# Gate on the accumulators between the third and the fourth step of a Strassen-type second projection, and the residual added in the fourth

## The chip, the core and the metric

The kernel runs on one core of one Trainium2 chip. The time is the device time of one execution in microseconds (us). The kernel before takes 2689.62 us, the median of three runs (2686.9 to 2690.53). TensorE multiplies matrices and writes to PSUM, VectorE, ScalarE and GpSimd (POOL in the rows) do the element-wise work, and all loads and stores are issued by SyncE's queue (SP).

## The reference

One decoder layer on 2048 rows of 1024 columns. The change touches the MLP behind the mixer; `x` is the normed row entering it, `gt2`, `sh2`, `sc2` come from the conditioning vector.

```python
x = layer_norm(ALPHA * x + gt1 * y, ln1_g, ln1_b)
h = x * (1.0 + sc2) + sh2
f = jnp.square(jax.nn.relu(h @ w_ff1)) @ w_ff2        # 1024 -> 4096 -> 1024
x = layer_norm(ALPHA * x + gt2 * f, ln2_g, ln2_b)
```

All of it is float32. The kernel reaches that accuracy with three matmuls for one: each operand is split into a rounded high part and the rest (`split`: ScalarE writes the high part, VectorE or GpSimd subtracts), and `mm3` multiplies high x high, low x high and high x low.

## The kernel before

The work on the MLP is cut into two halves of 1024 rows (`for half`). Each half goes through the first projection; after both, each goes through the second.

Both projections are multiplied as 2x2 blocks with seven products in place of eight (Strassen in Winograd's form): P1 to P7 are products of blocks or of sums and differences of blocks, and the four blocks of the result are sums of some of them. So P1 goes into block (0,0), and into others through the running sums.

**First projection** (`up`, lines 1058 to 1120). 16 blocks `c` of 256 of the 4096 columns run per half, in pairs that take turns product by product (`next(pair[y])`). A block has four PSUM banks X, Y, Z, W. In the order P1 P5 P6 P7 P3 P4 P2, X takes P1 and P2, Z takes P5 and P3, Y takes P6, W takes P7 and P4. Line 1098 copies X to `u`, line 1101 adds Y, line 1105 forms `v = u + Z` before P3 is added into Z, line 1108 adds W before P4 goes into W, and lines 1113 and 1118 form two more results. `act` applies ReLU and the square and writes to DRAM (`g_d`). The weight's four blocks are loaded raw, added or subtracted on GpSimd (line 1076; on VectorE for the first four blocks of columns) and split into `wh` and `wl`, of which the pool `w1p` holds five each. The activations' seven operands are made by `split_h`, which a loop runs through before the first block is traced; each has its own pool (`hs4`), and the string `HSO` gives the order in which the pools of this stage are opened. Pools are stacked in memory, so this order decides which tiles of the stage before (`p3`: the output projection with its layer norm, whose statistics lie in `sm3`) a pool's tiles lie over, and so what they wait for.

Beside this the second weight is prepared (`prep`, line 1124): 16 pieces of 1 MB are loaded, combined and split into the seven operands of each of four steps `s` (1024 of the 4096 rows each), and written to DRAM (`wt_d`). A list of slots spreads the pieces over the blocks.

**Second projection** (`down`, from line 1239 on). Per half, four steps `s` of seven products; a product is two half-products of 24 matmuls, and PSUM holds four row tiles of it at a time. For each half-product a weight operand is loaded (`wl`, five buffers), the activation operand is formed by a subtraction (line 1259) and split (`gp`, three buffers). Line 1297 adds each row tile of each product to an accumulator in SBUF (8 tiles of 128x1024, in 4 blocks or quarters `(i, j)` of 4 row tiles x 512 columns); line 1295 copies the first of them. In the last step the order is P1 P5 P6 P3 P2 P7 P4, else P7 stands before P2.

After the last step come, per row tile, the gate (line 1213), the residual (`residual`: a load of `z`, two operations on GpSimd, and the add of line 1214), the layer norm's statistics (line 189), and the output. In the last step of the second half four tiles are normalized on VectorE (lines 1227 and 1230), the others on ScalarE (1234) and GpSimd or VectorE (1235, 1236). For its last product P4, the gate and residual of tiles 4 to 7 are applied ahead, and the product is multiplied by the gate on its way (line 1280).

The order of each engine's instructions is chosen when the kernel is built, by a planner that goes by the order in which they are traced as priority and by its own estimate of durations. Each engine then executes its list in order. `tc.issue_after(wdma[-1])` puts a load into SP's queue behind the last weight load traced.

Of the kernel before, what the change touches and what calls it, by code (L numbers as in the profile page):

```python
# [51 lines left out]
HSO = 6, 4, "u", 5, 3, 2, "s", "o", 0, 1, "w"  # L52
# [7 lines left out]
WLS = "VV"  # L60
WOS = "wwww", "xxzz"
# [9 lines left out]
OV = 4  # L71
GB = 3
WLB = 5
PIECES = 8 * 7
OO = 2
# [42 lines left out]
def build(nc, tc, I, out, upto=9, dbg=None):  # L118
# [805 lines left out]
    p3 = ctx.enter_context(ExitStack())  # L924
    h2p = pool(p3, "h2p", 2)
# [9 lines left out]
    sm3 = pool(p3, "sm3", 4)  # L935
# [84 lines left out]
    p4 = ctx.enter_context(ExitStack())  # L1020
    psf = [pool(p4, f"psf{i}", 4, space=PSUM) for i in range(2)]


    p4a = p4.enter_context(ExitStack())
# [13 lines left out]
    def split_h(half, o):  # L1038
# [5 lines left out]
        for x, (name, src, sub) in enumerate((("P1", b11, None), ("P5", b12, (b12, b11)), ("P6", b12, (b22, b12)),  # L1044
                                              ("P7", b11, (b12, b11)), ("P3", b22, None), ("P4", b12, (b21, b12)),
                                              ("P2", b21, None))):
# [11 lines left out]
    def up(half, c, H):  # L1058
# [9 lines left out]
        for _ in range(n // 2 % 4):  # L1068
            x, z, y, w = (order.index(i) for i in "XZYW")
            order[y], order[z], order[w], order[x] = "X", "Z", "Y", "W"  # L1070
# [36 lines left out]
        prod("P3", a21, OP.subtract, "Z", False, (a12, a21))  # L1107
        V.tensor_tensor(v, v, ps["W"], op=OP.add)
        act(v, 1, 1)
        yield  # L1110
# [4 lines left out]
        yield  # L1115
        prod("P2", a12, None, "X", False)
# [3 lines left out]
        act(ps["X"], 0, 0)  # L1120
# [3 lines left out]
    def prep(u):  # L1124
        s, k = divmod(u, 4)
        b = hraw.tile([P, 2, D], F32, tag="raw", name=f"w2r{u}")
        Q.dma_start(b, I["w_ff2"][8 * s * P:(8 * s + 8) * P].rearrange("(i k p) c -> k p i c", i=2, p=P)[k])
        b11, b12, b21, b22 = (b[:, i, 512 * j:512 * j + 512] for i in range(2) for j in range(2))
# [15 lines left out]
    for _ in split_h(0, H):  # L1144
        pass
    for half in range(2):
        todo = work(range(8 * half, 8 * half + 8))
        slots = [i for i in range(7 * NCH) if half or i < 7 * NCH - 8]
        slots = slots[14:] if half else slots[12:]
        want = PIECES  # L1150
# [3 lines left out]
        for c in range(0, NCH, 2):  # L1154
            pair = [up(half, x, H) for x in (c, c + 1)]
            for x in range(7):
                for y in range(2):
# [31 lines left out]
    ztp = pool(p4b, "ztp", 2)  # L1189
    sm4 = pool(p4b, "sm4", 4)  # L1190
    NST = DFF // 1024
    acc = {}
    wdma = []
    gt2, ag1, ab1, g2, b2 = (c4.tile([P, D], F32, name=n) for n in ("gt2", "ag1", "ab1", "g2", "b2"))
    rows = (gt2, gt_d[1]), (ag1, I["ln1_g"]), (ab1, I["ln1_b"]), (g2, I["ln2_g"]), (b2, I["ln2_b"])
# [8 lines left out]
    def residual(half, t):  # L1204
        zt = ztp.tile([P, D], F32, tag="zt", name=f"zt{half}_{t}")
        with tc.issue_after(wdma[-1]):
            Q.dma_start(zt, z_d[4 * border[2 * half + t // 4] + t % 4])
# [8 lines left out]
    def finish(half, t):  # L1216
        tt = 4 * border[2 * half + t // 4] + t % 4
        f = acc[t]
        if half == 0 or t < 4:
            gate(f, residual(half, t))  # L1220
# [161 lines left out]
```

## Time and profile before

| what | us |
|---|---|
| median of three runs | 2689.62 |
| profiled execution | 2691.44 |
| its span, first to last instruction | 2689.6 |
| TensorE busy (matmul) | 2447.0 (91%) |
| VectorE busy | 1815.3 (67%) |
| ScalarE busy | 1209.6 (45%) |
| GpSimd busy | 1148.1 (43%) |
| mean granted clock of TensorE | 0.96 |
| first matmul of the first projection | 1301.6 |
| first matmul of the second projection | 1982.75 |

Busy time is the sum of the instructions' durations on an engine; it says nothing on whether the engine could have done without waiting, so the stages are read one by one in the rows below. In a row, the operation stands as `out<-in` by tile names: `u_X` is bank X of the first projection, `d_W` bank W of the second, `acc` an accumulator, `zt` the residual, `gt` the gate, `w2s` a piece of the second weight, `a` a raw activation block of the second projection.

### The profile page before, as it was taken

Reading aid. Unit: us, or ns where it says so; the run is one execution under the profiler, and the core shown is the slowest. Engines: PE = TensorE matmul, PEld = TensorE weight load, DVE = VectorE, ACT = ScalarE, POOL = GpSimd, SP = SyncE. Lnnn points to the kernel's source line nnn. Section 1 sums busy time; section 2 is a strip of 40 time slices with the busy share of each in tenths; the row PEclk is TensorE's granted clock in tenths of the full one; section 3 lists DMA queues with packets and bytes.
Section 4 is the critical chain, followed back from the end, with each engine's and each line's share of the span. In section 5 each row is a group of like instructions: output and inputs, shape, how many; then the busy total and the mean of one; then the engine's idle time right before and its main releaser. Section 6 shows DMA issues by size and latency. Waiting matters only on the chain.

```text
span 2689.6 us, 33970 instructions
## 1 busy us (share of the span) xinstructions
PE 2447.0 (91%) x11668; PEld 2028.9 (75%) x11668; DVE 1815.3 (67%) x2891; ACT 1209.6 (45%) x2349; POOL 1148.1 (43%) x1055
## 2 busy tenths in 40 slices
PE   5999999989999999799799998989989999799982
PEld 5887878877787877588587786867878887588871
DVE  8657675566767776644877649776445557965578
ACT  5653222257777777234565555655542112221110
POOL 4323546558788977333312336323300004810037
PEclk9999999989999999899899999999999999899995
DMA  9366341020202111556688626886266767476552
GB/s 325 139 218 203 106 137 37 32 80 23 64 20 60 33 49 57 168 179 227 222 300 281 225 102 206 304 277 226 102 256 247 301 252 267 179 291 261 191 188 78
DMA packets 203469, 464.71 MB, mean 173 GB/s; under 512 B 18584, under 2 KB 52760, under 8 KB 188960
## 3 DMA queue, kind: packets, MB, share of 16 engines
q1 hardware_dynamic: 203296, 462.54, 49.4%
q8 instruction: 92, 1.51, 0.2%
q14 instruction: 81, 0.66, 0.1%
HBM read 313.30 MB, written 149.17 MB: 172 GB/s over the span
## 4 chain that ended last, share of the span: by engine, by line
PE 62%; DVE 16%; DMA 10%; issue 5%; ACT 4%; POOL 2%; SPq 0%; DVEq 0%; ACTq 0%; POOLq 0%
DMA wt_d<-w2s 4%; PE d_W L132 4%; PE d_W L133 4%; PE d_W L134 4%; PE t L835 3%; DMA wad<-in_w_ada 2%; PE o L826 2%; PE o L828 2%; PE d_Z L134 2%; PE d_Z L133 2%; PE pj L134 2%; PE d_Z L132 2%; PE pj L132 2%; PE pj L133 2%; PE s L132 2%
## 5 line engine op out<-in xcount | busy, mean ns | idle before, releaser
L1076 POOL TENSOR_TENSOR w<-w,w 128x512 f32<-128x512 f32 x112 | 167.7, 1503 | 377.7 <-DVE w1l_P L129 234.2
L129 DVE TENSOR_TENSOR w1l_P<-w,w1h_P 128x512 fp32r<-128x512 f32 x224 | 194.6, 872 | 65.7 <-ACT w1h_P L126 64.4
L807 ACT ACTIVATE p<-s,nm 128x512 f32<-128x512 f32 (+3 forms) x320 | 196.6, 627 | 39.7 <-DVE nm L804 36.2
L802 DVE TENSOR_REDUCE mx<-s 128x1 f32<-128x512 f32 (+3 forms) x288 | 175.2, 620 | 54.0 <-PE s L134 51.2
L1208 POOL TENSOR_TENSOR zt<-zt,ag 128x1024 f32<-128x1024 f32 x16 | 44.1, 2762 | 355.6 <-DMA zt<-z_d 355.6
L851 POOL TENSOR_TENSOR tl<-tf,th 128x512 fp32r<-128x512 f32 x144 | 183.7, 1288 | 1.7
L126 ACT ACTIVATE w1h_P<-w 128x512 fp32r<-128x512 f32 x224 | 138.1, 622 | 97.4 <-PE u_Y L133 25.2
L835 PE MATMUL t<-ident,p 128*128 128x128 f32 x1088 | 165.0, 277 | 7.8 <-DVE tl L129 4.0
L835 PEld LDWEIGHTS t<-ident,p 128*128 128x128 f32 x1088 | 130.6, 142 | 33.0 <-ACT tf L846 6.1
L133 PE MATMUL pj<-wbl,hhb 128*128 128x512 f32 x384 | 151.3, 394 | 0.6 <-DVE wbl L129 0.6
L132 PE MATMUL pj<-wbh,hhb 128*128 128x512 f32 x384 | 150.8, 395 | 0.9 <-ACT wbh L126 0.5
L134 PE MATMUL pj<-wbh,hlb 128*128 128x512 f32 x384 | 151.4, 395 | 0.0
L132 PE MATMUL s<-kt,qt 96*128 96x512 f32 (+3 forms) x320 | 128.4, 401 | 12.4 <-ACT p L807 10.2
L129 DVE TENSOR_TENSOR w2s<-w2r,w2s 128x512 fp32r<-128x512 f32 x112 | 98.0, 876 | 57.7 <-ACT w2s L126 57.2
L132 PE MATMUL u_Z<-hh_P,w1h_P 128*128 128x512 f32 x256 | 104.9, 410 | 28.4 <-DVE v L1105 28.4
L826 PE MATMUL o<-th,v 128*128 128x512 f32 (+2 forms) x320 | 123.1, 389 | 5.0 <-DVE osum L862 4.2
L828 PE MATMUL o<-tl,v 128*128 128x512 f32 (+2 forms) x320 | 124.0, 396 | 3.2 <-DVE tl L129 1.8
L126 ACT ACTIVATE w2s<-w2r 128x512 fp32r<-128x512 f32 x112 | 70.2, 628 | 123.7 <-DMA wt_d<-w2s 103.9
L133 PE MATMUL s<-kt,qt 96*128 96x512 f32 (+3 forms) x320 | 118.8, 371 | 3.7 <-DVE kt L129 3.7
L134 PE MATMUL s<-kt,qt 96*128 96x512 f32 (+3 forms) x320 | 118.5, 371 | 0.0
L132 PE MATMUL psY<-wo_h,mh 128*128 128x512 f32 x256 | 101.1, 400 | 10.8 <-ACT wo_h L126 10.3
L129 DVE TENSOR_TENSOR tl<-t,th 128x512 fp32r<-128x512 f32 (+3 forms) x176 | 92.7, 539 | 26.9 <-ACT th L126 25.7
(377 smaller groups left out, 7750.0 us busy)
## 6 DMA issues: line engine op xcount, KB each, us to landing
wP<-wt_d SPq DMA_DIRECT2D x112, 1024.0 KB, 4.8
wt_d<-w2s SPq DMA_DIRECT2D x112, 512.0 KB, 3.9
w<-in_w_ff SPq DMA_DIRECT2D x128, 256.0 KB, 3.8
a<-g_d SPq DMA_DIRECT2D x32, 1024.0 KB, 7.2
g_d<-v SPq DMA_DIRECT2D x96, 256.0 KB, 4.5
wad<-in_w_ada SPq DMA_DIRECT2D x64, 256.0 KB, 3.0
w2r<-in_w_ff SPq DMA_DIRECT2D x16, 1024.0 KB, 7.1
x<-in_x SPq DMA_DIRECT2D x16, 512.0 KB, 7.9
```

The lines of the kernel that those rows point to most:

```text
L126: A.activation(hi, x, AF.Copy)
L129: lo_eng.tensor_tensor(lo, x, hi.bitcast(F32), op=OP.subtract)
L132: T.matmul(ps, sh, mh, start=start, stop=False, skip_group_check=more)
L133: T.matmul(ps, sh, ml, start=False, stop=False, skip_group_check=more)
L134: T.matmul(ps, sl, mh, start=False, stop=stop, skip_group_check=more)
L802: V.tensor_reduce(mx[:, j:j + 1], ps[:, :n], op=OP.max, axis=AX.X)
L807: A.activation(pt[:, :m], b[:, :m], AF.Exp, bias=nm, accum_out=rs[:, qi, j:j + 1])
L826: T.matmul(po[:, cs], w, th[:, cs], start=(done == 0), stop=False)
L828: T.matmul(po[:, cs], w, tl[:, cs], start=False, stop=(done == nk))
L835: T.transpose(tp[:, qi * P:(qi + 1) * P], pts[h, 4 * qb + qi, kb // 4][1][:, kb % 4 * P:(kb % 4 + 1) * P], ident)
L851: (V if mode == "C" else G).tensor_tensor(tl[:, cs], tf[:, cs], th[:, cs].bitcast(F32), op=OP.subtract)
L1076: (V if half == 0 and c < W1V else G).tensor_tensor(src, *sub, op=op)
```

## The change

It has five parts.

1. *Gate.* `gt2` is loaded when the MLP begins. Each quarter of the accumulators is multiplied by it once, in the step before the last, behind the product that completes the quarter there. What the last step adds must then be gated already: its weight rows (`s == NST - 1`) are multiplied by `gt2` column by column in `prep`.
2. *Residual.* In the last step, behind P1, P5, P6 and P3, the residual of one quarter each is loaded, scaled on GpSimd and added to the accumulators, in pieces of 128x512 (four buffers) in place of 128x1024 (two).
3. The special path for the last P4 loses its gate, and `finish` begins with the statistics. The order "row tile by row tile" of P4's matmuls stays.
4. *Order of the first projection.* P2 goes ahead of P3 and P4: P1 P5 P6 P7 P2 P3 P4. The banks' order for the next block, the pools' order and two buffer counts (v 4 to 3, r 2 to 1) go with it.
5. *Entry.* The seven operands of the first half are traced one by one, each ahead of the product that needs it in the first pair of blocks. `sm3` is opened as the first pool of the stage before. The last weight pieces are to be finished ten slots earlier.

```diff
-HSO = 6, 4, "u", 5, 3, 2, "s", "o", 0, 1, "w"
+HSO = 6, 5, "u", 4, 3, 2, "s", "o", 0, 1, "w"
+RES = dict(P1=(0, 1), P5=(1, 1), P6=(0, 0), P3=(1, 0))
-OV = 4
+OV = 3
-OO = 2
+OO = 1
...
     p3 = ctx.enter_context(ExitStack())
+    sm3 = pool(p3, "sm3", 4)
...
-    sm3 = pool(p3, "sm3", 4)
...
+    gt2p = pool(p4, "gt2p", side="right")
+    gt2 = gt2p.tile([P, D], F32, name="gt2")
+    rowbc(gt2, gt_d[1])
...
-            order[y], order[z], order[w], order[x] = "X", "Z", "Y", "W"
+            order[y], order[x], order[z], order[w] = "X", "Z", "Y", "W"
...
+        prod("P2", a12, None, "X", False)
         V.tensor_tensor(v, v, ps["W"], op=OP.add)
         act(v, 1, 1)
+        yield
+        prod("P3", a21, OP.subtract, "Z", False, (a12, a21))
+        act(ps["X"], 0, 0)
         yield
         prod("P4", a22, None, "W", False)
...
+        if s == NST - 1:
+            for i in range(2):
+                V.tensor_tensor(b[:, i], b[:, i], gt2, op=OP.mult)
+            yield
...
-    for _ in split_h(0, H):
-        pass
+    first = split_h(0, H)
...
-        slots = slots[14:] if half else slots[12:]
-        want = PIECES
+        slots = slots[14:-10] if half else slots[12:]
+        want = 8 * 7 + 4 * half
...
+                if half == 0 and c == 0:
+                    next(first, None)
...
+    def quarter(half, i, tp, j):
+        return acc[4 * i + tp][:, 512 * j:512 * j + 512]
+
+    def gate(half, i, j):
+        for tp in range(4):
+            c = quarter(half, i, tp, j)
+            V.tensor_tensor(c, c, gt2[:, 512 * j:512 * j + 512], op=OP.mult)
+
+    def residual(half, i, j):
+        cs = slice(512 * j, 512 * j + 512)
+        for tp in range(4):
+            zt = ztp.tile([P, 512], F32, tag="zt", name=f"zt{half}_{i}{j}{tp}")
+            with tc.issue_after(wdma[-1]):
+                Q.dma_start(zt, z_d[4 * border[2 * half + i] + tp][:, cs])
+            G.tensor_tensor(zt, zt, ag1[:, cs], op=OP.mult)
+            G.tensor_tensor(zt, zt, ab1[:, cs], op=OP.add)
+            c = quarter(half, i, tp, j)
+            V.tensor_tensor(c, c, zt, op=OP.add)
...
     def finish(half, t):
-        if half == 0 or t < 4:
-            gate(f, residual(half, t))
...
             if half == 1 and last and name == "P4":
                 ops = [parts(q) for q in range(2)]
                 for tp in range(4):
-                    gate(acc[4 + tp], residual(half, 4 + tp))
-                for tp in range(4):
                     for k in range(4):
                         mm(tp, k, *ops[k // 2])
-                    y = ztp.tile([P, D], F32, tag="zt", name=f"y{tp}")[:, 0:512]
-                    V.tensor_tensor(y, ps[ch, tp], gt2[:, 0:512], op=OP.mult)
-                    V.tensor_tensor(acc[4 + tp][:, 0:512], acc[4 + tp][:, 0:512], y, op=OP.add)
-                return
...
+                if s == NST - 2 and (name, i, j) in (("P2", 0, 0), ("P3", 0, 1), ("P7", 1, 1), ("P4", 1, 0)):
+                    gate(half, i, j)
+            if last and name in RES:
+                residual(half, *RES[name])
```

## Rows read from the trace of the kernel before

**Rows 1.** Table of stretches: length, busy us per engine (count), granted clock, DMA share, GB/s.

```profile
1700.00:1800.00 100.00, 89.11 (x380) 72.64 (x379) 76.54 (x102) 55.24 (x99) 25.03 (x16) 0.96 0.83 283
...
2250.00:2360.00 110.00, 88.32 (x347) 69.59 (x347) 101.07 (x90) 31.03 (x35) 87.18 (x41) 0.91 0.61 224
...
2474.00:2549.00 75.00, 75.00 (x333) 62.10 (x332) 42.02 (x48) 14.07 (x14) 0.00 (x0) 1.00 0.54 197
...
2549.00:2604.00 55.00, 55.00 (x244) 45.56 (x243) 38.50 (x44) 11.99 (x12) 12.87 (x7) 1.00 0.59 211
...
2604.00:2622.00 18.00, 10.84 (x48) 8.63 (x46) 18.00 (x14) 1.95 (x2) 12.46 (x5) 0.89 0.32 114
...
2622.00:2636.00 14.00, 13.63 (x48) 10.93 (x48) 14.00 (x13) 0.00 (x0) 13.92 (x8) 0.78 0.12 40
...
2636.00:2690.00 54.00, 0.26 (x2) 0.00 (x0) 45.87 (x46) 3.61 (x3) 34.52 (x22) 0.52 0.23 87
```

**Rows 2.** Timeline of TensorE, 2614 to 2623 us: start, length, instruction, [idle before].

```profile
2614.46 0.39 PE L134 MATMUL d_W<-wP,gP7l 128*128 128x512 f32 x1
...
2622.37 0.77 PE L132 MATMUL d_W<-wP,gP4h 128*128 128x512 f32 x1 [7.53 <-issue]
```

**Rows 3.** Timeline of VectorE, end of the last step.

```profile
2621.61 0.66 DVE L1297 TENSOR_TENSOR acc<-acc,d_W 128x512 f32<-128x512 f32 x1
...
2685.13 1.40 DVE L1230 SCALAR_TENSOR_TENSOR acc<-acc,rs,b 128x512 f32<-128x512 f32 x2
```

**Rows 4.** Groups by form, 2592 to 2690 us: busy us, mean ns, idle before.

```profile
L1214 DVE TENSOR_TENSOR acc<-acc,zt 128x1024 f32<-128x1024 f32 x8 | 18.2, 2276 | 4.6 <-POOL zt L1209 4.5
L1213 DVE TENSOR_TENSOR acc<-acc,gt 128x1024 f32<-128x1024 f32 x8 | 17.1, 2158 | 0.0
...
L1280 DVE TENSOR_TENSOR y<-d_W,gt 128x512 f32<-128x512 f32 x4 | 2.7, 684 | 0.1
...
L189 DVE BATCH_NORM_STATS2 st<-acc 128x6 f32<-128x512 f32 x16 | 10.1, 674 | 0.0
```

**Rows 5.** Instructions on the accumulators: ns shortest/median/longest, first and last start.

```profile
L1297 DVE TENSOR_TENSOR acc<-acc,d_W x100: 625/687/689, 2037.2 to 2623.5; 128x512 f32<-128x512 f32 x100
...
L1213 DVE TENSOR_TENSOR acc<-acc,gt x16: 1210/1933/3422, 2260.3 to 2631.7; 128x1024 f32<-128x1024 f32 x16
...
L1227 DVE SCALAR_TENSOR_TENSOR acc<-acc,mv,g x8: 737/740/2831, 2640.3 to 2684.5; 128x512 f32<-128x512 f32 x8
```

**Rows 6.** Waits of TensorE, 1280 to 1980 us: total, times, longest.

```profile
PE u_Z L132 <- DVE v L1105: 28.4, 7, 7.2
...
PE psT L965 <- ACT z L1001: 12.8, 2, 8.6
```

**Rows 7.** Timeline of VectorE and TensorE at 1798 us.

```profile
1798.05 0.68 DVE L1105 TENSOR_TENSOR v<-u,u_Z 128x512 f32<-128x512 f32 x1
...
1798.87 0.77 PE L132 MATMUL u_Z<-hh_P,w1h_P 128*128 128x512 f32 x1 [5.17 <-DVE v L1105]
```

**Rows 8.** Waits of ScalarE, 1300 to 1980 us.

```profile
ACT w2s L126 <- DMA wt_d<-w2s: 103.9, 67, 4.5
```

**Rows 9.** Instructions of line 1076 on GpSimd.

```profile
L1076 POOL TENSOR_TENSOR w<-w,w x112: 1280/1519/2381, 1375.5 to 1940.6; 128x512 f32<-128x512 f32 x112
```

**Rows 10.** Timeline of SP's queue, from 2538 us.

```profile
2538.72 38.40 SPq L1257 DMA_DIRECT2D wP<-wt_d  x8
```

**Rows 11.** Groups by form, 2236 to 2362 us, the change of half.

```profile
L1259 DVE TENSOR_TENSOR a<-a,a 128x1024 f32<-128x1024 f32 x8 | 20.7, 2605 | 0.0
...
L1213 DVE TENSOR_TENSOR acc<-acc,gt 128x1024 f32<-128x1024 f32 x8 | 15.1, 1908 | 0.0
```

**Rows 12.** Groups by form, 1980 to 2236 us.

```profile
L1259 DVE TENSOR_TENSOR a<-a,a 128x1024 f32<-128x1024 f32 x31 | 37.7, 1224 | 1.7 <-DMA a<-g_d 1.0
```

**Rows 13.** Timeline of ScalarE at the entry.

```profile
1299.55 1.24 ACT L1001 ACTIVATE z<-z,nm,rs 128x1024 f32<-128x1024 f32 x1 [4.12 <-DVE nm L200]
...
1300.70 2.17 ACT L126 ACTIVATE w1h_P<-w 128x512 fp32r<-128x512 f32 x4
```

More of the change, by code (lines that the diff above doesn't have):

```diff
@@ L70 @@
 W1B = 5
-OV = 4
+OV = 3
 GB = 3
 WLB = 5
-PIECES = 8 * 7
-OO = 2
+OO = 1
 W1U = 2
@@ L1020, in build @@
     p4 = ctx.enter_context(ExitStack())
+    NST = DFF // 1024
     psf = [pool(p4, f"psf{i}", 4, space=PSUM) for i in range(2)]
+    gt2p = pool(p4, "gt2p", side="right")
+    gt2 = gt2p.tile([P, D], F32, name="gt2")
+    rowbc(gt2, gt_d[1])
     p4a = p4.enter_context(ExitStack())
@@ L1044, in split_h @@
         for x, (name, src, sub) in enumerate((("P1", b11, None), ("P5", b12, (b12, b11)), ("P6", b12, (b22, b12)),
-                                              ("P7", b11, (b12, b11)), ("P3", b22, None), ("P4", b12, (b21, b12)),
-                                              ("P2", b21, None))):
+                                              ("P7", b11, (b12, b11)), ("P2", b21, None), ("P3", b22, None),
+                                              ("P4", b12, (b21, b12)))):
             p = hs4[x]
@@ L1106, in up @@
         yield
-        prod("P3", a21, OP.subtract, "Z", False, (a12, a21))
+        prod("P2", a12, None, "X", False)
         V.tensor_tensor(v, v, ps["W"], op=OP.add)
         act(v, 1, 1)
+        yield
+        prod("P3", a21, OP.subtract, "Z", False, (a12, a21))
+        act(ps["X"], 0, 0)
         yield
@@ L1114, in up @@
         act(v, 0, 1)
-        yield
-        prod("P2", a12, None, "X", False)
         v = o("v", "v")
@@ L1119, in up @@
         act(v, 1, 0)
-        act(ps["X"], 0, 0)
     def prep(u):
@@ L1188, in build @@
     wl = pool(p4b, "wl", WLB)
-    ztp = pool(p4b, "ztp", 2)
+    ztp = pool(p4b, "ztp", 4)
     sm4 = pool(p4b, "sm4", 4)
-    NST = DFF // 1024
     acc = {}
     wdma = []
-    gt2, ag1, ab1, g2, b2 = (c4.tile([P, D], F32, name=n) for n in ("gt2", "ag1", "ab1", "g2", "b2"))
-    rows = (gt2, gt_d[1]), (ag1, I["ln1_g"]), (ab1, I["ln1_b"]), (g2, I["ln2_g"]), (b2, I["ln2_b"])
+    ag1, ab1, g2, b2 = (c4.tile([P, D], F32, name=n) for n in ("ag1", "ab1", "g2", "b2"))
+    rows = (ag1, I["ln1_g"]), (ab1, I["ln1_b"]), (g2, I["ln2_g"]), (b2, I["ln2_b"])
     def load_rows():
@@ L1202, in load_rows @@
             G.tensor_scalar(t, t, ALPHA, 0.0, op0=OP.mult, op1=OP.add)
[L1204 to L1207, printed above, removed]
-        G.tensor_tensor(zt, zt, ag1, op=OP.mult)
-        G.tensor_tensor(zt, zt, ab1, op=OP.add)
-        return zt
-    def gate(f, zt):
-        V.tensor_tensor(f, f, gt2, op=OP.mult)
-        V.tensor_tensor(f, f, zt, op=OP.add)
+    def quarter(half, i, tp, j):
[14 more added lines that the diff above has]
+            V.tensor_tensor(c, c, zt, op=OP.add)
     def finish(half, t):
```

## The prediction

> **What bounds the kernel now.** I read the table of stretches first. From 2474 to 2604 us TensorE is busy in all of the time at granted clock 1.00, the upper of its two levels, 2.4 GHz [rows 1]; there nothing but fewer matmuls could shorten the span. 333 recorded matmuls in 75 us are 0.225 us each. The second projection loses time mostly in two places. Around the change of half (2250 to 2360) 347 matmuls, 78 us of work, take 110 us: 32 us lost, with VectorE busy in 101 and GpSimd in 87. At the end TensorE stops at 2614.7, waits 7.5 us, runs 14 us for its last 48 matmuls at mean clock 0.78, and from 2636 to the end only VectorE and GpSimd work [rows 1, 2].
>
> Next I read what VectorE does there. It adds the seventh product's first tile at 2621.6 [rows 3] although TensorE had it done at 2614.7, and the fourth product, which adds into the same bank, starts right behind, at 2622.4 [rows 2]. So VectorE's backlog is the bound from about 2605 on: 8 gate multiplies, 17.1 us, and 8 residual adds, 18.2 us, with the 8 statistics pairs and the output's multiplies behind them [rows 4]. The gate multiply takes 1.21 us at its fastest and 3.42 at its slowest; the add of a PSUM bank never takes over 0.689 [rows 5]. So an operation whose two inputs lie in SBUF is stretched when GpSimd works, and one with a PSUM input is not.
>
> For the first projection I read TensorE's waits: 28.4 us in seven waits for line 1105, the longest 7.2 us at the entry, and 12.8 us at the entry for the layer norm before it [rows 6]. At 1798 line 1105 runs in VectorE's order behind the splits of the second weight [rows 7], whose ScalarE half waits 103.9 us in all for the write of an earlier piece [rows 8].
>
> **The end of the last step.** Gate multiplies (17.1 us) and residual adds (18.2 us) leave VectorE's last 90 us, and the four multiplies with the gate of line 1280 (2.7 us) go too [rows 4]: 38 us, and the wait for GpSimd's residual operand with it. Then the backlog is gone and the fourth product follows the seventh at once: 2614.8 + 48 x 0.225 = 2625.6. What remains late is the chain per row tile: add 0.69, two statistics 2 x 0.67, aggregate 0.2: 2.2 us, and for the three tiles finished on VectorE four operations of 0.74 more [rows 4, 5]: 5.2 us. The product completes its row tiles one by one, 2.7 us apart, the first at 2617.5; VectorE needs 2.2 + 3 x 5.2 = 17.8 us and ends at 2635.3, plus 3 for the first four tiles' remains and for the multiply of the one tile on GpSimd beside them, plus 3.1 from VectorE's last operation (2686.5) to the end: 2641 to 2642 against 2689.6. Gain 48, I take 47 (bounds 35, if GpSimd stretches all twelve operations as now, and 51).
>
> **The residual in the fourth step.** It doesn't vanish: per half 16 loads of 256 KB, 32 GpSimd operations on 128x512 and 16 adds. GpSimd's nearest row is 1.28 us at its fastest, 1.52 median [rows 9]: 41 to 49 us. The weight loads run five buffers ahead in SP's queue (eight issued in 38 us [rows 10]), the new loads stand right behind them, so GpSimd starts some 22 us before the product that names them and works from about 2540 to 2590. In this stretch VectorE has some ten splits and eight subtractions of 1.22 us [rows 12] and now 16 adds of 0.68: 33 us with both inputs in SBUF, beside PSUM adds that nothing stretches. VectorE now is 38.5 busy of 55 [rows 1]; with the adds 49.5, and with a stretch of 0.5 to 1 us on each of 34 operations 66 to 83. It falls 11 to 28 us behind; three operand buffers hold about 11 us of TensorE's work. The price is 0 to 17 us per half; I take 10, so 20, near the middle because the row nearest to it, the subtraction, 1.22 us before the change of half [rows 12], is stretched to 2.6 there by GpSimd operations twice as wide [rows 11]. What is queued behind such an add on VectorE is the next operand's split, and TensorE waits for that.
>
> The Trainium skill, page "SBUF — State Buffer", section "Who interferes with whom", says that the pair of ports is locked whole: an operation of VectorE with two SBUF inputs and one of GpSimd that reads SBUF block one another fully. By that rule GpSimd's 41 to 49 us and VectorE's 33 stand one after the other, 74 to 82 us in 55, and the price is 8 to 16 after the buffers; by its middle the estimate of the whole would be 2612. The rows that bear on it agree in kind: 2.6 against 1.22 us [rows 11, 12], and 0.689 at most with a PSUM input [rows 5].
>
> **The gate after the third step.** 16 multiplies of 0.69 us per half, 11 us, go into a step in which VectorE is busy 42.0 of 75 us and GpSimd 0 [rows 1]: nothing on the path. If that cover were gone they would cost their 11. The gate on the last weight rows is eight multiplies of 1.22 us, 9.8 us, in a stretch where VectorE has 23 of 100 us free [rows 1]: nothing, at most 5 by waiting for the raw weight's load in VectorE's order.
>
> **The change of half.** 32 us lost [rows 1]. 15.1 us of gate, 8 residual adds and 16 GpSimd operations leave it [rows 11]; statistics, normalization and GpSimd's two output operations stay. I take 25 of the 32 back (15 to 28); the residual's price above is already counted against it.
>
> **The order of the first projection.** No matmul is added or removed. Line 1105 must read bank Z before the third product adds into it; now the second product stands between, two blocks of 12 matmuls, 5.4 us. The six waits outside the entry (28.4 - 7.2 = 21.2 us, one of 5.2 at 1798 [rows 7]) fit under that. Each is also followed by slow matmuls: from 1700 to 1800 380 matmuls are 86 us of work, 14 us lost, of which 11 idle [rows 1]; 21.2 x 1.3 = 28. One buffer less for v and for r makes an activation wait for a write now and then. ScalarE's waits for the written pieces stay and what they delay may be another split: I take 22 (5 to 28).
>
> **The entry.** The first weight split starts at 1300.7, the moment the layer norm's last activation has read its statistics [rows 13], and by the order of pools the split's buffers lie over the statistics'. After the change these buffers lie elsewhere, so block 0 can start while TensorE now waits 12.8 us [rows 6]. The second block's banks and u's memory still wait for the transposes. I take 8 (0 to 13).
>
> **Sum.** 47 - 20 + 25 + 22 + 8 = 82. The profiled execution took 2691.44 us, 1.8 more than the median of 2689.62: 2691.44 - 82 - 1.8 = 2607.6, so 2608.
>
> **Rivals.**
> A. *The end gives part of it back* (0.21): VectorE is late out of the fourth step and stays so through the last three products, so that the price of the residual is 17 in both halves and the end loses 15 more of its gain: 2608 + 14 + 15 = 2637. For it: VectorE had no idle time from 2604 to 2636 [rows 1]. Against: most of that load is what goes.
> B. *The waits on line 1105 move* (0.14): ScalarE's 103.9 us [rows 8] reach TensorE through the weight split instead: gain 5 and not 22, entry 2 and not 8: 2631. Against: the splits run several products ahead, line 1105 doesn't.
> C. *All of it is hidden* (0.17): residual at no cost, 28 in the first projection, 12 at the entry, 28 at the change of half, 49 at the end: 2608 - 20 - 6 - 4 - 3 - 2 = 2573.
> D. *Slower* (0.06): VectorE executes in the written order, and each of 32 residual adds stands there before GpSimd's two operations are done. If each stops it for the pair at 1.95 us, halfway from the median 1.52 to the longest 2.38 [rows 9], that is 32 x 3.9 = 125 us in place of the 20 taken: 2713. It decides from 102 us, 3.2 us for each add. For it: VectorE did wait 4.5 us for one such operand [rows 4]. Against: loads are two products ahead.
> E. *The residual stays at the end* (0.04): its loads sit in SP's queue behind weight loads that wait for buffers, GpSimd starts 40 us later, and only the gate's share of the end is won, 20 in place of 47: 2635.
>
> **How the numbers follow.** The forecast has 0.38, with its own range 2590 to 2622. From 2568 to 2655 it holds the forecast, A, B, E and most of C, and leaves out D and the far sides of C and A. 0.2% (5 us) is about what a measurement of this kernel tells from no change. D is slower; a little of A and D ends near nothing. Faster 0.92, same 0.02, slower 0.06.
>
> **What would show it.** Right: TensorE's last matmul within 3 us of the seventh product's end plus 10.8; no gate multiply in the last step; GpSimd busy over 35 us in the 60 us before the second product and VectorE's subtractions there over 1.8 us; waits on line 1105 under 8 us in sum; under 8 us idle around the change of half behind the fourth step. Wrong: waits of TensorE for splits of the fourth step over 15 us per half, waits of VectorE for the residual operand over 10 us, or more than 45 us from the last matmul to the end.

## The result: 2664.8 us, 25 us faster, where 82 were forecast

The changed kernel takes 2664.76 us (median of 4, 2659.0 to 2667.16) beside 2689.47 before (4 runs on the same chip): ratio 0.9906, 95% interval 0.9889 to 0.9924, that is 20 to 30 us. The forecast was 2608, its range 2568 to 2655: the sign is right, the size is not. The profiled execution took 2665.75 us, its span 2663.9.

The two timelines, cut so that each line holds the same work in both (336 matmuls are four of the first projection's 32 blocks; changes are taken before rounding):

| stage | before | after | change | forecast |
|---|---|---|---|---|
| up to the last matmul before the MLP | 1286.0 | 1288.0 | +1.9 | 0 |
| from there through 336 matmuls of the first projection | 104.5 | 117.5 | +13.1 | -8 |
| the first projection's other 2352 matmuls | 583.9 | 589.1 | +5.3 | -22 |
| to the first matmul of the second projection | 8.4 | 2.8 | -5.6 | 0 |
| second projection on TensorE | 653.5 | 651.9 | -1.6 | -15.6 |
| last matmul to the end | 53.4 | 14.6 | -38.8 | -36.4 |

In the last column the forecast's 47 for the end stands in two lines: the last matmul 10.6 us earlier (2636.2 to 2625.6), and the other 36.4 behind it; the residual (+20) and the change of half (-25) are in the fifth line. So the tail came as computed. Lost were 21 us at the entry, 27 in the rest of the first projection and 14 in the second; the 5.6 at its start were not foreseen.

Below, some stretches are cut at u copies (ScalarE's read of a block's bank X; blocks count from 0). Such a cut does not always hold equal work: the copy of block 4 starts behind 363 of the 2688 matmuls before and behind 390 after, and 27 matmuls are 6.1 us. Times between u copies are compared only where the product order is the same.

The table of stretches of the kernel after, columns as in [rows 1]:

```profile
1700.00:1800.00 100.00, 88.85 (x371) 69.68 (x370) 80.56 (x103) 53.54 (x96) 29.60 (x19) 0.98 0.77 267
2250.00:2360.00 110.00, 100.21 (x427) 81.43 (x427) 104.23 (x109) 34.88 (x39) 73.33 (x44) 0.95 0.66 238
2474.00:2549.00 75.00, 75.00 (x333) 62.10 (x332) 51.52 (x60) 14.86 (x14) 6.55 (x4) 1.00 0.58 205
2549.00:2620.00 71.00, 58.50 (x248) 47.01 (x247) 66.59 (x62) 9.92 (x10) 49.68 (x31) 0.95 0.52 191
2620.00:2649.00 29.00, 25.56 (x106) 20.64 (x105) 27.04 (x38) 7.68 (x7) 20.10 (x16) 0.94 0.29 109
2649.00:2664.00 15.00, 0.31 (x2) 0.00 (x0) 11.87 (x17) 0.00 (x0) 6.21 (x6) 0.66 0.37 140
```

The third line is the third step with the gate in it: VectorE has 51.5 us where it had 42.0, TensorE still misses nothing. The fourth is where the residual now lies: GpSimd 49.7 us, VectorE 66.6 of 71, and TensorE 12.5 us short. The last is what is left of the 54 us tail. The kernel after enters its second projection 14.7 us later than the kernel before, so the second line is not the same work as in [rows 1]; the steps themselves are compared further down.

Waits of TensorE from 1280 to 1980 us, answering [rows 6] (total, times, longest):

```profile
PE u_Z L134 <- DVE w1l_P L129: 14.9, 11, 4.3
PE u_X L134 <- DVE w1l_P L129: 10.6, 11, 2.8
PE u_Y L134 <- DVE w1l_P L129: 10.4, 6, 3.8
PE psT L965 <- ACT h2f L967: 5.8, 3, 4.9
...
PE u_X L132 <- ACT u L1102: 4.7, 1, 4.7
PE u_W L134 <- DVE w1l_P L129: 2.2, 2, 1.6
```

and, before, the waits for the low half of a split weight:

```profile
PE u_X L134 <- DVE w1l_P L129: 4.0, 3, 2.7
PE u_Y L134 <- DVE w1l_P L129: 3.4, 1, 3.4
PE u_Z L134 <- DVE w1l_P L129: 2.2, 1, 2.2
```

The 28.4 us for the read of bank Z are gone without a rest. 38.1 us for the low half of a split weight stand in their place (9.6 before). Without the entry, from the u copy of block 4 to that of block 31, TensorE waited 31.8 us before and 34.4 after.

Instructions answering [rows 5] and [rows 9]: ns shortest/median/longest, first and last start:

```profile
L1229 DVE TENSOR_TENSOR acc<-acc,zt x32: 669/1746/1782, 2223.6 to 2616.4; 128x512 f32<-128x512 f32 x32
L1226 POOL TENSOR_TENSOR zt<-zt,ag x32: 1258/1731/2239, 2217.8 to 2610.0; 128x512 f32<-128x512 f32 x32
L1304 DVE TENSOR_TENSOR acc<-acc,d_W x104: 665/683/689, 2051.7 to 2654.1; 128x512 f32<-128x512 f32 x104
L1218 DVE TENSOR_TENSOR acc<-acc,gt x32: 684/686/1784, 2194.4 to 2566.2; 128x512 f32<-128x512 f32 x32
```

A residual add, which reads two tiles of SBUF, takes 1.75 us in the middle and 0.67 at best. The add of a PSUM bank beside it never passes 0.689.

### The profile page after: what moved, and what is told of

The parts are those of the page before. It is cut to its first block, busy times and chain, and to the rows that moved or that the text cites. A ratio compares the mean times of both kernels' runs of the same rounds, so it can differ in the third digit from the quotient of the medians.

```text
span 2663.9 us, 34047 instructions
## 1 busy us (share of the span) xinstructions
PE 2453.7 (92%) x11668; PEld 2020.8 (76%) x11668; DVE 1816.5 (68%) x2927; ACT 1202.8 (45%) x2349; POOL 1160.7 (44%) x1087
## 4 chain that ended last, share of the span: by engine, by line
PE 58%; DVE 16%; DMA 13%; issue 5%; ACT 5%; POOL 3%; SPq 1%; DVEq 0%; ACTq 0%; POOLq 0%
DMA wt_d<-w2s 6%; PE t L835 3%; PE d_W L134 3%; PE d_W L132 3%; PE d_W L133 3%; DMA wad<-in_w_ada 2%; PE psY L133 2%; PE psY L134 2%; PE psY L132 2%; PE pj L134 2%; PE pj L132 2%; PE o L826 2%; PE pj L133 2%; PE o L828 2%; PE s L132 2%
## 5 line engine op out<-in xcount | busy, mean ns | idle before, releaser
L129 DVE TENSOR_TENSOR w1l_P<-w,w1h_P 128x512 fp32r<-128x512 f32 x224 | 202.6, 907 | 76.0 <-ACT w1h_P L126 75.3
L1226 POOL TENSOR_TENSOR zt<-zt,ag 128x512 f32<-128x512 f32 x32 | 52.5, 1652 | 307.2 <-DMA zt<-z_d 307.2
L126 ACT ACTIVATE w2s<-w2r 128x512 fp32r<-128x512 f32 x112 | 70.3, 629 | 150.3 <-DMA wt_d<-w2s 137.2
L134 PE MATMUL u_Z<-hh_P,w1l_P 128*128 128x512 f32 x256 | 102.9, 402 | 14.9 <-DVE w1l_P L129 14.9
L134 PE MATMUL u_X<-hh_P,w1l_P 128*128 128x512 f32 x256 | 102.8, 402 | 10.8 <-DVE w1l_P L129 10.6
```

The lines of the kernel that those rows point to most:

```text
L126: A.activation(hi, x, AF.Copy)
L129: lo_eng.tensor_tensor(lo, x, hi.bitcast(F32), op=OP.subtract)
L134: T.matmul(ps, sl, mh, start=False, stop=stop, skip_group_check=more)
```

## The experiments

The order is that of the questions: the entry, the product order, the residual, then what sets the pace of the first projection. Times are medians; each ratio is to the kernel before on the same chip, with its interval. The kernel before took 2686.1 to 2690.6 on the five chips used, so a difference of a few us between runs of different chips decides nothing. A diff is against the changed kernel unless it says otherwise.

**e1: the entry's operands traced at once, as before**

```diff
-    first = split_h(0, H)
+    for _ in split_h(0, H):
+        pass
...
-                if half == 0 and c == 0:
-                    next(first, None)
```

> The changed kernel with all seven operands of the first half traced ahead of the first block again; all else as changed. Theory A (tracing in turn puts the first weight splits ahead of the last layer norm in VectorE's order, so that its last activation starts at 1314.3 and not 1299.6, and the transposes, the banks of the second block and u's memory follow 15 to 20 us later): the last layer-norm activation is back before 1303, the second block's copy of X (1348.5 changed, 1328.9 before) at about 1330, and the time falls by 15 to 20 us from 2664.8 to about 2647. Theory B (what matters is that the splits' buffers no longer lie over the statistics, in whatever order it is traced): no change, 2660 to 2667, the layer norm still after 1310.

2659.32 us, 0.9890 [0.9873, 0.9906]; the changed kernel has 0.9906. The last activation of the layer norm starts at 1315.7 (after: 1314.3), the u copy of block 1 at 1347.1 (after: 1348.5). The order of tracing isn't what costs the entry.

**e2: sm3 opened as the last pool again**

```diff
     p3 = ctx.enter_context(ExitStack())
-    sm3 = pool(p3, "sm3", 4)
...
     x3 = pool(p3, "x3", 2)
+    sm3 = pool(p3, "sm3", 4)
```

> The changed kernel with the statistics' pool opened last in its stage again, so that the first weight splits' buffers lie over other tiles; the operands are still traced in turn. Theory B (place of the statistics): the splits wait for the layer norm, which is back before 1303; 2645 to 2652. Theory A (order of tracing): no gain, 2660 to 2667.

2644.78, 0.9832 [0.9819, 0.9846]: 20 us faster than the changed kernel. ScalarE at the entry, first after, then e2:

```profile
1282.41 1.14 ACT L126 ACTIVATE w1h_P<-w 128x512 fp32r<-128x512 f32 x2
...
1304.29 1.24 ACT L1001 ACTIVATE z<-z,nm,rs 128x1024 f32<-128x1024 f32 x1 [2.10 <-DVE nm L200]
...
1314.30 1.24 ACT L1001 ACTIVATE z<-z,nm,rs 128x1024 f32<-128x1024 f32 x1 [0.70 <-DVE nm L200]
```

```profile
1301.67 1.24 ACT L1001 ACTIVATE z<-z,nm,rs 128x1024 f32<-128x1024 f32 x1 [4.12 <-DVE nm L200]
1302.82 1.65 ACT L126 ACTIVATE w1h_P<-w 128x512 fp32r<-128x512 f32 x3
```

And VectorE of the kernel after:

```profile
1283.06 3.18 DVE L129 TENSOR_TENSOR w1l_P<-w,w1h_P 128x512 fp32r<-128x512 f32 x2 [0.24 <-ACT w1h_P L126]
...
1292.00 3.43 DVE L129 TENSOR_TENSOR w1l_P<-w,w1h_P 128x512 fp32r<-128x512 f32 x2
...
1298.40 0.63 DVE L997 TENSOR_TENSOR z<-psY,axl 128x512 f32<-128x512 f32 x1
```

Before, the first weight split waited for the statistics to be read [rows 13], and that wait kept it behind the last tile's layer norm. With the wait gone, the splits of the first weights run ahead: four low halves, 6.6 us, stand ahead of the last add into z (line 997 here), which starts at 1298.40 where before it started at 1289.87, and its layer norm ends 15 us later. Its transposes, the banks of block 1 and u's memory follow. In e2 the u copy of block 1 starts at 1327.24, in after at 1348.47, and the first 336 matmuls are done after 105.9 us, 104.5 before the change and 117.5 with it.

**e4: the old product order, with everything else of the change**

```diff
-HSO = 6, 5, "u", 4, 3, 2, "s", "o", 0, 1, "w"
+HSO = 6, 4, "u", 5, 3, 2, "s", "o", 0, 1, "w"
...
-        prod("P2", a12, None, "X", False)
+        prod("P3", a21, OP.subtract, "Z", False, (a12, a21))
...
```

> The changed kernel with the first projection's products in the old order P1 P5 P6 P7 P3 P4 P2 (bank order and pool order with it); buffer counts, tracing in turn, gate and residual as changed. Theory M (the order only moves TensorE's waits from line 1105 to the weight splits, whose pace is set by ScalarE waiting for the writes of the second weight's pieces): 2658 to 2672, waits on the sum with Z back at 15 us or more and on the splits down by as much. Rival O (the order itself is worth its 21 us and the loss lies in the fewer buffers or the entry): 2680 or more.

2666.55, 0.9919 [0.9904, 0.9934]: no difference to the changed kernel. Waits of TensorE in e4, 1280 to 1995 us:

```profile
PE u_Z L132 <- DVE v L1109: 27.0, 13, 5.0
PE d_W L132 <- ACT gP1h L126: 8.5, 1, 8.5
```

The wait on bank Z is back with all its 27 us, and the time doesn't move: the new order had only moved the wait to the splits. In the first projection's last 2352 matmuls the old order is even 5.5 us shorter (583.6 us, 589.1 after). At the start of the second projection the old order waits 8.5 us, the new one 2.8, and the first step behind it takes 82.1 us, 77.9 after.

**e8: gate and residual alone (old entry, old place of sm3, old order)**

The edits are those of e4, e2 and e1 together; the gate in `prep`, the slots and the buffer counts stay as changed.

> Gate, residual and last product as changed (with the prep's gate, slots and buffer counts), but the entry, the statistics' pool and the products' order as before. If the gate's part is worth what the traces say (tail 38 us shorter, second projection 2 us shorter, entry and first projection no better or worse than before): 2690 - 40 = 2650. If the order of the first projection was worth its 21 us after all: 2665 or more, since its waits come back without the entry's gain.

2656.29, 0.9883 [0.9865, 0.9901]: the gate and residual alone are worth 31 us, at least as much as the whole change (25; the two intervals overlap). The entry's 336 matmuls take 104.7 us, the other 2352 take 585.0 (104.5 and 583.9 before): the gate on the weight rows and the fewer buffers cost about 1 us in the traces.

**e3: the residual without GpSimd**

```diff
-            G.tensor_tensor(zt, zt, ag1[:, cs], op=OP.mult)
-            G.tensor_tensor(zt, zt, ab1[:, cs], op=OP.add)
```

> The changed kernel without the two GpSimd operations of the residual: scale and bias of the residual are left out, loads and adds stay. Theory P (the price of the residual in the fourth step is GpSimd holding VectorE's second input): the adds fall from 1.75 to 0.69 us, TensorE's 18 us lost in the fourth step of the first half and 20 in the second fall under 5 each, time about 2635. Rival L (it is VectorE's load, 16 adds more and the gates, whatever GpSimd does): at least half of the loss stays, 2648 or more.

2632.94, 0.9788 [0.9773, 0.9802]: 32 us faster than after. Waits of TensorE from 1990 us, first after, then e3:

```profile
PE d_X L132 <- issue: 15.9, 2, 8.6
PE d_Z L134 <- DVE gP5l L129: 7.6, 3, 4.9
PE d_W L132 <- issue: 3.4, 1, 3.4
```

```profile
PE d_W L132 <- issue: 4.5, 1, 4.5
PE d_W L132 <- DMA wP<-wt_d: 2.7, 1, 2.7
PE d_Z L134 <- DVE gP3l L129: 1.2, 1, 1.2
```

The adds are still there, 0.69 us each in place of 1.75, and so are the loads; scale and bias are left out. Without GpSimd's 64 operations the long waits of the fourth step vanish: a step of 336 matmuls takes 76.2 us where nothing waits, the fourth steps of the two halves 94.2 and 96.8 after, 76.2 and 83.2 in e3. The 7.3 and 8.6 us are P2 waiting for banks; the profile names no releaser for them. VectorE's order gives one: the add that empties the first of these banks stands behind residual adds, the last of which waits for GpSimd, and P2 starts 0.1 us after that add. From the kernel after:

```profile
2607.14 1.73 DVE L1229 TENSOR_TENSOR acc<-acc,zt 128x512 f32<-128x512 f32 x1 [1.16 <-POOL zt L1227]
2608.80 1.27 DVE L1304 TENSOR_TENSOR acc<-acc,d_Z 128x512 f32<-128x512 f32 x2
2609.58 0.77 PE L132 MATMUL d_X<-wP,gP2h 128*128 128x512 f32 x1 [8.56 <-issue]
```

One part of the forecast's schedule failed too: SP's queue in the last step of the kernel after, and what its residual loads wait for from 2540 to 2640 us,

```profile
2559.41 18.70 SPq L1270 DMA_DIRECT2D wP<-wt_d  x4
2584.84 5.55 SPq L1225 DMA_DIRECT2D zt<-z_d  x4
...
SPq L1225 <- DVE acc L1229: 31.0, 12, 6.6
```

The last of the four weight loads leaves at 2577.8; the residual's third four loads then wait 6.6 us more, and one after the other for the residual adds of P5's quarter (from 2584.13), because the residual has four buffers, one quarter's worth. GpSimd sits idle until 2587.5 (16.2 us), and its work bunches from there to 2614, where it was put at 2540 to 2590.

**e6: the residual spread over third and fourth step; e7: e6 and e2 together**

```diff
-RES = dict(P1=(0, 1), P5=(1, 1), P6=(0, 0), P3=(1, 0))
+RES = {(2, "P3"): (0, 1), (2, "P2"): (1, 1), (3, "P1"): (0, 0), (3, "P6"): (1, 0)}
...
-            if last and name in RES:
-                residual(half, *RES[name])
+            if (s, name) in RES:
+                residual(half, *RES[s, name])
```

> The changed kernel with the residual's four quarters spread over two steps: behind P3 and P2 of the third step and P1 and P6 of the fourth, in place of P1, P5, P6 and P3 of the fourth. Theory P (the price is GpSimd's operations standing close together on VectorE's second input, and banks freed late): TensorE's loss of 18 us in the fourth step of the first half and of 20 in the second falls to about 6 each, 2640. Rival: the third step now loses what the fourth did, since the gate's multiplies stand there: no gain, 2658 or more.

> The residual spread as in the run beside it and the statistics' pool opened last again: both gains add if they are in separate places: 2640 - 20 = 2620. If either theory is wrong, 2640 or more.

e6 2643.91, 0.9831 [0.9814, 0.9848]; e7 2628.81, 0.9779 [0.9763, 0.9795]. The same 64 GpSimd operations and 32 adds, 21 us cheaper where they bunch less. The adds in e7:

```profile
L1229 DVE TENSOR_TENSOR acc<-acc,zt x32: 677/682/1778, 2183.0 to 2566.7; 128x512 f32<-128x512 f32 x32
```

The median is 0.682 and no longer 1.746: 10 of the 32 adds take over 1 us, 22 in the kernel after. In e7 the two gains, 20 and 21, nearly add up (36); 2620 had been expected.

**e5: half of the writes of the second weight's pieces left out**

```diff
-            Q.dma_start(wt_d[s][x][k // 2][:, :, k % 2], t.bitcast(F32))
+            if s < 2:
+                Q.dma_start(wt_d[s][x][k // 2][:, :, k % 2], t.bitcast(F32))
...
-                wdma.append(Q.dma_start(w.bitcast(F32), wt_d[s][x][q]).ins)
+                wdma.append(Q.dma_start(w.bitcast(F32), wt_d[s % 2][x][q]).ins)
```

> The changed kernel without the writes of the second weight's pieces in the second half of the first projection (the last two steps of the second projection then read the first two steps' pieces); the pieces are still loaded, combined, gated and split. Theory W (the pace of the first projection is set by ScalarE standing in its order for these writes, whatever the order of products): the 249 us between the copies of X of blocks 17 and 28 fall to 215 or less (11 blocks of 84 matmuls are 209), time about 2635. Rival V (VectorE's load beside GpSimd sets it): 235 us or more, 2655 or more.

2655.67, 0.9873 [0.9855, 0.9891], 9 us. ScalarE's waits for these writes fall from 137.2 us to 72.0; the u copies of blocks 17 to 28, where writes are left out, come 235.7 us apart, 248.9 in after, 209.5 at TensorE's pace (11 x 84 matmuls of 0.2267 us). So a third of the loss is due to the writes; as sole cause of the pace they are refuted (215 us or less were expected for that). What is left led to e9.

**e9: e7 without GpSimd's weight sums; e11: these sums on VectorE; e12: half of them**

```diff
e7:
             if sub:
                 (V if half == 0 and c < W1V else G).tensor_tensor(src, *sub, op=op)
e9:
             if sub and half == 0 and c < W1V:
                 V.tensor_tensor(src, *sub, op=op)
e11:
             if sub:
                 V.tensor_tensor(src, *sub, op=op)
e12:
             if sub:
                 (V if half == 0 and c < W1V or name in ("P5", "P3") else G).tensor_tensor(src, *sub, op=op)
```

> This is e7 (residual spread over the third and fourth steps, sm3 opened last) without GpSimd's sums and differences of the first projection's weights, from the fifth chunk of the first half on and in the whole second half; so these products work on unsummed weights, and the time is read without the 112 or so additions. What they tell apart: what sets the pace of the first projection, where the u copies of blocks 4 to 31 come 541 us apart in every version against 27 x 19.04 = 514 us at TensorE's pace. Theory P: VectorE's subtractions and splits there have two SBUF inputs and are stretched by GpSimd's additions; without them VectorE's residue operation falls from about 0.9 to under 0.75 us, blocks 4 to 31 take 514 to 522 us and the time falls from 2628.8 to 2602 to 2612. Theory V: it is VectorE's own load together with ScalarE's wait for the written pieces; VectorE's work is the same, blocks 4 to 31 take 533 to 541 us, and the time stays at 2621 to 2631. The additions also go from the path raw weight, sum, split; as they run ahead by chunks this is put at nothing by both.

> e7 with all sums and differences of the first projection's weights on VectorE (112 move from GpSimd); nothing is left out. From e9: without GpSimd there, VectorE is 311 us busy of the 510 from 1440 to 1950 instead of 363, and the time is 22 lower. Theory S (the stretch is the cost): the additions come back as 98 x 0.69 = 68 us of VectorE in that stretch, to 379 of 510, all unstretched, and the reserve suffices: blocks 4 to 31 take 522 to 532 us (e7 544), the time is 2606 to 2620. Theory L (VectorE's load is the cost, by whichever way it comes): 379 is more than 363, and the sum now stands in VectorE's order ahead of the split: blocks 4 to 31 take 541 to 555, the time 2626 to 2642.

> e7 with the weight sums of the products P5 and P3 (two of four in each chunk) on VectorE, the others on GpSimd as before; nothing is left out. VectorE: 311 + half of the stretch (26) + 49 x 0.69 (34) = 371 us busy of 510. Theory S: half of what e11 gains if e11 gains: 2616 to 2626. Theory L: 2627 to 2640. If GpSimd's additions cost only where two of them follow each other, e12 gains as much as e11.

e9 2606.57, 0.9698 [0.9680, 0.9717]; e11 2610.86, 0.9712 [0.9698, 0.9726]; e12 2620.45, 0.9747 [0.9731, 0.9764]. Blocks 4 to 31: 544.3 us in e7, 521.8 in e9, 524.7 in e11, 538.2 in e12. Groups and stretch from 1440 to 1950 us, e7:

```profile
L129 DVE TENSOR_TENSOR w1l_P<-w,w1h_P 128x512 fp32r<-128x512 f32 x172 | 161.2, 941 | 64.2 <-ACT w1h_P L126 61.6 <-DMA g_d<-v 2.0
L129 DVE TENSOR_TENSOR w2s<-w2r,w2s 128x512 fp32r<-128x512 f32 x79 | 69.4, 882 | 45.5 <-ACT w2s L126 45.2
...
1440.00:1950.00 510.00, 476.07 (x2027) 382.06 (x2026) 362.82 (x436) 281.61 (x488) 185.15 (x113) 0.99 0.64 216
```

and e11:

```profile
L129 DVE TENSOR_TENSOR w1l_P<-w,w1h_P 128x512 fp32r<-128x512 f32 x176 | 130.1, 743 | 52.5 <-ACT w1h_P L126 52.2
L1080 DVE TENSOR_TENSOR w<-w,w 128x512 f32<-128x512 f32 x97 | 67.0, 698 | 11.3 <-DMA w<-in_w_ff 9.4 <-DVE w1l_P L129 0.9
L129 DVE TENSOR_TENSOR w2s<-w2r,w2s 128x512 fp32r<-128x512 f32 x76 | 52.2, 688 | 33.3 <-ACT w2s L126 33.3
...
1440.00:1950.00 510.00, 490.01 (x2107) 395.79 (x2106) 369.55 (x538) 287.56 (x496) 32.23 (x11) 0.99 0.64 217
```

97 more operations, 67.0 us, and VectorE is 6.7 us busier: the rest is what GpSimd's 153 us had taken from it. The theory of the stretch holds, and the load alone is refuted: e11 has the larger load and the shorter time. That the sums merely reached the splits earlier is not what the traces show: in this stretch ScalarE's half of the split waits for GpSimd's sums 4.0 us in all in e7, and for VectorE's 14.7 us in e11. ScalarE's waits for the written pieces did not change either (88.9 us in e7, 87.6 in e11). e11 leaves nothing out and is the fastest version that does so: 78 us faster than before.

The Trainium skill, page "Perfetto Trace Analysis", section "Optimizing Scalar/DVE Operations", says that moving work between VectorE and GpSimd might not help, as they share a read port. These rows agree: the 153 us that GpSimd took over had spared VectorE 6.7.

**e10: e8 with the residual spread; e13: e10 with the sums on VectorE; e14: the kernel before with the sums on VectorE**

```diff
(e13 against e10, e14 against the kernel before)
-                (V if half == 0 and c < W1V else G).tensor_tensor(src, *sub, op=op)
+                V.tensor_tensor(src, *sub, op=op)
```

> The kernel of e8 (gate after the third step and residual in the steps of the second projection, but the entry, the place of sm3 and the product order of the first projection as before the change) with the residual spread as in e6. Beside e7 it differs only in the product order of the first projection with its bank order and the entry traced in turn. Theory M: the order is worth nothing and the entry's tracing nothing, so the times differ only by the start of the second projection, where the old order waits 8.5 us in place of 2.8: e8 less the 12 to 21 that the spread gave, 2635 to 2644, thus 6 to 15 over e7. Theory O: the new order does gain in the first projection what was predicted (22), which the entry's loss had covered: 2650 or more. If spread and order hinder each other (the new order's advantage is a loss once the entry is right), e10 comes at or below e7, 2628 or less.

> e10 (old product order and old tracing of the entry, residual spread) with the weight sums on VectorE; it differs from e11 by the product order of the first projection and the entry's tracing. Theory C (the order's gain was real and covered): without the stretch the waits on bank Z, 33 us in e10, stay 25 to 33 us, because the read of Z still stands in VectorE's order behind a split, while e11 has 14 us of waits for w1l: e13 is 15 to 25 over e11, 2626 to 2636, and the sums on VectorE bring it only 1 to 11 against e10. Theory N (the order is worth 8 whatever the splits cost): 2617 to 2622, and the waits on Z fall to half, as the split ahead of the read is shorter.

> The kernel before the change with nothing but its weight sums on VectorE instead of GpSimd; it leaves nothing out. Theory C: the waits on line 1105 (28.4 us) set the pace there, and the stretch lies under them: 0 to 10 faster, 2679 to 2690. Theory N: the stretch sets it, as in e7, 15 to 20 faster: 2669 to 2675.

e10 2637.02, 0.9801 [0.9784, 0.9818], as expected of an order that is worth no more than the start of the second projection: 6 to 8 over e7. In the traces the old order waits 6.3 us more there and its first step takes 4.4 more, while the first projection's last 2352 matmuls take 588.7 us in e10 and 590.6 in e7. e13 2621.89, 0.9766 [0.9754, 0.9779]: over e11 11 us by the medians, 14.5 by the ratios, between the two theories; the waits are those of the one, the time is nearer to the other. Waits of TensorE, 1300 to 1995 us, in e13:

```profile
PE u_Z L132 <- DVE v L1109: 26.3, 7, 6.2
PE d_W L132 <- ACT gP1h L126: 8.3, 1, 8.3
```

and in e11, 1280 to 1980:

```profile
PE u_Z L134 <- DVE w1l_P L129: 7.5, 6, 2.8
PE u_Z L132 <- ACT w1h_P L126: 5.3, 1, 5.3
PE u_X L132 <- ACT w1h_P L126: 3.1, 1, 3.1
PE u_X L134 <- DVE w1l_P L129: 2.6, 4, 1.3
PE d_W L132 <- DMA wP<-wt_d: 2.5, 1, 2.5
```

Without the stretch, too, 26 us on bank Z become 24 us on the weight's two halves (18.5 in the lines above, the rest in smaller ones). The last 2352 matmuls take 569.4 us in e13 and 568.3 in e11; the difference comes behind them: 5.8 us of waiting for the second projection and 7.0 in its first step (83.8 and 76.8). e14, 2673.05, 0.9952 [0.9939, 0.9964], is 13 us faster: the stretch was there before the change, under the waits on line 1105 (blocks 4 to 31 527.6 for 545.7). From 1440 to 1950 us in e11 ScalarE still waits 87.6 us for written pieces and 81.5 before weight splits, 39 of these for matmuls of banks Y and W; which of these waits reaches TensorE, once GpSimd is quiet, stays open.

## Why the prediction was wrong, step by step

**The end of the last step: right, but for its last product.** From the end of the seventh product to the end of the kernel 74.8 us became 30.8: 44 gained, 47 forecast. The fourth product's start answers [rows 2], and two stretches behind it (columns as above) show the granted clock, all of the kernel after:

```profile
2636.58 0.68 PE L132 MATMUL d_W<-wP,gP4h 128*128 128x512 f32 x1 [3.44 <-issue]
```

```profile
2636.50:2640.00 3.50, 3.42 (x8) 2.76 (x9) 3.50 (x4) 0.00 (x0) 3.42 (x2) 0.52 0.33 127
2640.50:2649.00 8.50, 8.50 (x39) 6.95 (x37) 8.03 (x14) 1.25 (x1) 3.44 (x6) 1.00 0.31 123
```

The wait fell from 7.53 to 3.44 us and not to nothing, and behind it 8 matmuls run at granted clock 0.52, the lower level, until it is 1.00 again. So the last matmul ends 16.2 us behind the seventh product, where 10.8 was computed and 3 more allowed: this sign failed. The wait isn't GpSimd's, it is 4.5 us in e3. The tail behind the last matmul, 14.6 us, is 2.4 shorter than forecast.

**The gate after the third step: right.** Nothing on the path [third line of the table above]. Its last four multiplies slipped into the fourth step, beside the residual, and took 1.63 us each; that none would run there had been a sign of being right. In e3, without GpSimd's residual, the first half's fourth step loses nothing, these multiplies included.

**The change of half: right.** Its two steps, the first half's fourth and the second half's first, took 83.7 and 100.3 us before, 31.6 over twice 76.2. Without GpSimd's residual (e3) they take 76.2 and 79.3, 3.1 over: 28.5 came back, 25 were forecast. In the kernel after they take 94.2 and 78.3, and the 18 us of the former are the residual's.

**The residual: a term mis-sized.** Forecast 20 (0 to 34), measured 32 by e3, near the upper bound: 18.0 us in the first half's fourth step and 13.6 in the second's. Three things in its working were off. The residual adds are stretched by 1.06 us in the middle (0.68 to 1.75), past the 0.5 to 1 allowed. The subtractions, for which over 1.8 was announced, took 1.40 in the last fourth step. The operand's split was named as what TensorE would wait for; it waited mainly for banks. The announced signs of failure did not appear: waits for splits 11.2 us in the whole second projection, waits of VectorE for the operand 3.5, so these were the wrong signs. And the step that set the schedule failed: the loads were to run with the weight loads, five buffers ahead, but the residual has four buffers of its own, and the third quarter's loads waited for the adds of the second. So the work bunched from 2587.5 to 2614, around P2's start at 2609.6. The price is that of rival A's first half (17 in both halves), without its loss at the end; rival E's mechanism, loads held by weight loads alone, is not what the trace shows. e6 shows that two thirds of the price is the bunching. By the Trainium skill's rule on the locked ports, weighed in the prediction (page "SBUF — State Buffer", section "Who interferes with whom"), 8 to 16 a half were worked out; 18.0 and 13.6 came, its upper end in sum. The rule, not the middle between ends, was the better estimate.

**The order of the first projection: wrong.** "The six waits outside the entry fit under that" was true, no such wait is left, but each us of TensorE's wait was credited as time. In the last 2352 matmuls of the first projection the new order is 5.5 us longer than the old in the change (e4), 1.9 longer with the entry mended (e7, e10) and 1.1 shorter with GpSimd quiet (e11, e13): it was worth nothing there. What it was worth in the whole time, 2 (inside the noise), 8 and 11 us by the medians, lies at the start of the second projection and was not forecast; why the old order starts it later is not shown. The pace came from the weight splits, stretched by GpSimd's sums (22 of 590.6 us, e7 to e11) and held by ScalarE's in-order waits for the written pieces (13 of 589.1 us, after to e5). This is rival B, which had 0.14 and gave the term 5: its counter-argument, that the splits run several products ahead, was the failing step. The rows to see it were there: ScalarE's 103.9 us [rows 8], and 1.5 us GpSimd additions [rows 9] beside operations with two SBUF inputs, the same pair that the forecast did price in the second projection.

**The entry: wrong in sign.** Forecast -8 (-13 to 0), measured +13.1, of which e2 takes back 11.6; the rest of its gain (18 us between the two traces, 20 by the medians) lies elsewhere. The step that failed: a wait removed was taken for time won. That wait kept the first weight splits out of VectorE's and ScalarE's order ahead of the layer norm on which the next blocks depend. What these queues would do first in its place was not asked.

In sum 21 (entry), 27 (order), 14 (second projection: about 12 residual and 5 last product, less 3 at the change of half) and 2 ahead of the MLP, less 6 at the start of the second projection and 2 at the tail: 56 us between the profiled executions, 57 between 2608 and the median of 2665.

## What to carry to other kernels

Where a wait is removed on an in-order engine, list what now runs earlier on it and who stands behind that: a wait can be what keeps the urgent work first. Credit a removed wait of the bound engine only with the distance to the next-late wait, and look for that in the other engines' waits of the same stretch. And before work is placed on GpSimd, count VectorE's operations with two SBUF inputs beside it: spreading it (21 us) or giving it back to VectorE (18 us) each won nearly as much here as the change itself (25). And cut two timelines where equal work is done, not at an instruction that the planner may move: by the u copies the entry seemed to lose 23 us and the first projection to gain 5.

## What the runs showed of the hardware that was not expected

An addition of 128x512 moved from GpSimd to VectorE cost VectorE next to nothing: 97 of them, 67.0 us, raised its busy time from 362.8 to 369.6, as the low halves of the splits fell from 0.941 to 0.743 us and the pieces from 0.882 to 0.688. The stretch also depends on bunching: the median of the same 32 residual adds is 1.746 us in one placement and 0.682 in the other. And it is mutual: where the kernel after runs three residual adds (from 2598.66) against three of GpSimd's operations (from 2599.85) they alternate, each 1.70 to 1.78 us long, where an add takes 0.68 alone and GpSimd's operation 1.26 at best; so a pair passes in 1.7 us, not far below the 1.94 of one behind the other.
